# First weight loads in smaller pieces, and the squares and norm steps of the first projection moved back

## The chip, the cores and the metric

The kernel runs on one core of one Trainium2 chip, which has five engines: TensorE (PE in the profile; PEld is its weight load), VectorE (DVE), ScalarE (ACT), GpSimd (POOL) and SyncE (SP, which here only issues transfers). The metric is the time on the device in microseconds; lower is better.

## The reference

One layer of a streaming encoder over T = 1072 tokens in one list: 16 meta tokens, 1024 prompt frames, 32 frames of a running stream. What matters here is its beginning:

```python
def rmsnorm(x, g):
    r = rsqrt(mean(x * x, -1) + EPS)
    return (x * r) * g

z = rmsnorm(x, norm_mix) @ w_in              # (T, 1024) @ (1024, 1792)
a_in, q, k, v = split(z, [1024, 1536, 1664])
glu = a_in[:, :512] * sigmoid(a_in[:, 512:])
# depthwise conv (width 31) over glu, layer norm, swish   -> A
# sliding-window attention over q, k, v                   -> B
x = x + concat([A, B]) @ w_out
# then a gated feed-forward with a conv of width 3, a residual, and a last rmsnorm
```

All data is float32.

## The kernel before

**Layout.** Channels lie on the 128 partitions and tokens on the free axis, so x is 8 slices of 128 channels (k = 0 to 7), in three blocks of tokens, TB: block 0 has 336, block 1 384, block 2 352. w_in is cut into 14 chunks of 128 output columns, `win[c]`, each with 8 slices of 128 rows.

**Three products for one.** Each operand is split into a rounded high part and a remainder, both float32r: ACT makes the high part, DVE the remainder (`split` for weights, lines L246 and L247; L338 and L339 for x, which also multiply by the norm's gain). The tiles are `whi`, `wlo` for weights and `hi`, `lo` (HI[b], LO[b]) for x. A **step** is one slice k of one chunk and one block: three matmuls (L252 high by high, L253 high weight by low x, L254 low weight by high x). Eight steps in a row add up one chunk of one block in one PSUM bank.

**The first 48 steps.** `START` lists them: chunks 0 and 1 of block 0 step by step in turn (steps 0 to 15), then chunk 0 of block 1 (16 to 23), chunk 0 of block 2 (24 to 31), chunk 1 of block 1 (32 to 39), chunk 1 of block 2 (40 to 47). From step 48 on the main loop takes the other chunks, each for blocks 0, 1, 2; its first is chunk 2 (48 to 55 for block 0, 56 to 63, 64 to 71). A counter, `slot`, numbers the steps. Before step 0 PE runs WRM = 18 matmuls on ones (L319), which need no input. Three PSUM banks, tag `mm`, hold in turn chunk 0 and chunk 1 of block 0 and chunk 0 of block 1; tags `o`, `pt0` and `pt1` hold the other three sums. Step 48 takes the first `mm` bank again, once chunk 0 of block 0 has been read out.

**The norm comes late.** The projection runs on x times gain, and its result is multiplied by `rb[b]`, the tokens' 1/rms, on the way out of PSUM (DVE, L572 and the lines by it). For rb[b], ACT squares each slice of x (L359, into `sqs` buffers, six of them), DVE adds them up (L362), and `rms_first` runs in three parts, each called behind a step that `RM[b]` names: column sums by six PE instructions (L268, out `R`) with DVE and POOL work for the power -0.5 (L271, L275 to L279); three ACT multiplications into `diag` (L283); six PE instructions that spread the result (L289, out `R`) and an ACT copy into rb (L349).

**What sets the order.** PE's instructions follow the text. ACT's follow it from the main loop on; before that, ACT's, and DVE's, SP's and POOL's throughout, are put in order by a planner that takes what it thinks is ready, earlier in the text first. `tc.issue_after(ins)` puts an instruction behind `ins` on the same engine. `SQB[b]` = (b', k) puts block b's squares behind ACT's cast of slice k of block b', `SQD[b]` its additions behind DVE's remainder of that slice. Conv taps (L397, L400) fill DVE where nothing else is ready.

**Later weights.** A chunk from the main loop on comes by one transfer of 512 KB (L231); ACT writes the high part (L237) and the negated copy (L241), and a transfer that POOL issues adds the raw weights to that (L242). Chunks 0 and 1 own both buffers of `raw`, `whi` and `wlo`, so chunk 2 waits until chunk 0 is used up (step 31).

Of the kernel before, what the change touches and what calls it, by code (L numbers as in the profile page):

```python
# [18 lines left out]
P = 128  # L19
# [39 lines left out]
PF = 7  # L59
START = (((0, 0), (1, 0)), ((0, 1),), ((0, 2),), ((1, 1),), ((1, 2),))  # L60
WRM = 18
FS = 1
LASTK = ((0, 1), (1, 3), (3, 5), (5, 8))
ENDN = 448
# [36 lines left out]
DN = 264  # L101
FORD = (0, 1, *range(2, 10, 2), *range(3, 10, 2), *range(10, 18, 2), *range(11, 18, 2), 18, 19, 20, 21)
NSUM = 1
SQB = ((1, 7), (2, 7), (2, 7))
SQD = ((0, 7), (2, 7), (2, 7))
RM = ((27, 31, 41), (45, 48, 53), (56, 59, 63))
VR = 16
BW = SEG + 2 * NMETA
SSW = 128 + NS + NMETA + 1
# [14 lines left out]
def build():  # L124
# [35 lines left out]
    with tile.TileContext(nc, schedule_with_timeline_sim=True) as tc:  # L160
        with tc.tile_pool(name="cons", bufs=1) as cp, tc.tile_pool(name="wp", bufs=2) as wp, \
                tc.tile_pool(name="xp", bufs=1) as xp, tc.tile_pool(name="dr", bufs=1, space=DRAM) as dp:
            body(nc, tc, cp, wp, xp, dp, locals())
# [3 lines left out]
def body(nc, tc, cp, wp, xp, dp, io):  # L167
# [3 lines left out]
    d = _N()  # L171
# [18 lines left out]
    def pcol(name, i):  # L190
        o, _ = PRM[name]
        return prm[:, o + i:o + i + 1]
# [52 lines left out]
    def split(hi, lo, src):  # L245
        nc.scalar.copy(hi, src)  # L246
        nc.vector.tensor_tensor(out=lo, in0=src, in1=hi.bitcast(F32), op=ALU.subtract)  # L247
# [69 lines left out]
    hid, cast = {}, {}  # L317
    for i in range(WRM):
        nc.tensor.matmul(warm[:, 0:P], ones, ones, start=True, stop=True)  # L319

    nc.scalar.dma_start(prm, d.prm)
    for b, (t0, n) in enumerate(TB):
        if b == 0:
            pre = [[wp.tile([P, 1024], F32 if t == "raw" else F32R, tag=t, name=t) for t in ("raw", "whi", "wlo")]
                   for c in range(2)]
        for k in range(0, KD, 2):
            if b == 0 and k % 4 == 0:
                for c in range(2):
                    raw, hi, lo = (z[:, k * P:k * P + 512] for z in pre[c])
                    nc.sync.dma_start(raw, d.win[c, :, k:k + 4].rearrange("p a b -> p (a b)"))  # L330
                    split(hi, lo, raw)
            nc.sync.dma_start(X[b][:, k:k + 2, :], d.xT[:, k:k + 2, t0:t0 + n])
        if b == 0:
            pre = [z[1:] for z in pre]
        if b == 0:
            nc.scalar.dma_start(ident, d.cst[:, 0, :])
        for k in range(KD):
            hid[b, k] = nc.scalar.activation(HI[b][:, k, :], X[b][:, k, :], AF.Copy, scale=pcol("g1", k)).ins  # L338
            cast[b, k] = nc.vector.scalar_tensor_tensor(out=LO[b][:, k, :], in0=X[b][:, k, :], scalar=pcol("g1", k),  # L339
                                                        in1=HI[b][:, k, :].bitcast(F32), op0=ALU.mult,  # L340
                                                        op1=ALU.subtract).ins
# [11 lines left out]
    for b, (t0, n) in enumerate(TB):  # L353
        parts = [acc[:, p, t0:t0 + n] for p in (1, 0)[:NSUM]]
        for k in range(KD):
            sq = pd.tile([P, 384], F32, tag="sqs", name="sq", bufs=6)[:, :n]
            to = parts[k % NSUM] if k < NSUM else sq
            with tc.issue_after(hid[SQB[b]]):
                nc.scalar.activation(to, X[b][:, k, :], AF.Square)  # L359
            if k >= NSUM:  # L360
                with tc.issue_after(cast[SQD[b]]):
                    nc.vector.tensor_tensor(out=parts[k % NSUM], in0=parts[k % NSUM], in1=sq, op=ALU.add)  # L362
# [184 lines left out]
    def in_mm(b, w, lead=0):  # L547
# [3 lines left out]
        for k in range(KD):  # L551
            mm3(ps, [k], lambda k: hv[:, k, :], lambda k: lv[:, k, :], lambda k: HI[b][:, k, lead:],
                lambda k: LO[b][:, k, lead:], k == 0, k == KD - 1)
            for g, at in zip(rms1, RM):
                if slot[0] in at:
# [446 lines left out]
    a, z = None, None  # L1002
# [3 lines left out]
    for i in range(len(jobs) + 2):  # L1006
# [34 lines left out]
        z, a = a, job  # L1041
# [159 lines left out]
    with tc.tile_pool(name="psB", bufs=1, space=PSUM, reuse_waits="tile") as pf:  # L1201
# [346 lines left out]
        def d_mm(ps, w, rows, t0, n):  # L1548
            at = t0 - NMETA
            mm3(ps, range(len(rows)), lambda k: w[0][:, k * P:k * P + P], lambda k: w[1][:, k * P:k * P + P],  # L1550
                lambda k: rows[k][0][:, at:at + n], lambda k: rows[k][1][:, at:at + n])
# [141 lines left out]
        for pos, (t0, n) in enumerate(ENDS):  # L1693
            last = pos + 1 == len(ENDS)
            for m in range(KD):
                ps = mmt()[:, :n]
                d_mm(ps, [z[:, m % 2] for z in wend[m // 2]], crow, t0, n)
                if pos and FS <= m < FS + 3:
                    next(fin, None)
# [10 lines left out]
                elif m:  # L1710
                    parts.append(to)
                if pos and m >= FS + 3:
                    next(fin, None)
# [103 lines left out]
```

## Time and profile before

| | |
|---|---|
| median of 3 runs | 1063.87 us (1062.63 to 1065.57) |
| profiled execution, its own time | 1064.06 us |
| its span, first to last instruction | 1062.3 us |
| mean granted TensorE clock | 0.996 of full speed |
| PE busy | 1037.6 us, 98% of the span |
| DVE busy | 865.6 us, 81% |
| ACT busy | 508.6 us, 48% |

The span is what the rows' times count in; 1.8 us of the execution lie around it. PE's busy time is that of overlapping matmuls, so gaps are read from the starts of successive matmuls.

### The profile page before, as it was taken

To read this page: it belongs to the slowest core of one execution; us is meant where nothing else is said; L and a number is where in the kernel's file an instruction comes from. 1 tells how busy PE (TensorE), PEld (TensorE's weight loads), DVE (VectorE), ACT (ScalarE), POOL (GpSimd) and SP (SyncE) were. 2 spreads that over 40 slices of the span, in tenths; PEclk is the share of its full clock that TensorE was granted. 3 is DMA by queue.
4 is the path that set the end of the run, shared out by engine and by line. 5 is a ranking of instruction groups with operands and counts; after the bars stand their busy time and mean duration, and the time that the engine had idled before them with its cause. 6 is when DMAs were issued, how large, how long until landed. Compare 5 with 4: busy or idle time off the path is not lost.

```text
span 1062.3 us, 19939 instructions
## 1 busy us (share of the span) xinstructions
PE 1037.6 (98%) x7741; PEld 1010.0 (95%) x7741; DVE 865.6 (81%) x1643; ACT 508.6 (48%) x1068; POOL 173.4 (16%) x203
## 2 busy tenths in 40 slices
PE   9999999889999999999999999999999999999996
PEld 9999997658999999999999999999999999999996
DVE  7999997899978988878888887888778766985636
ACT  8653436897675644333333343443336622532333
POOL 1132120002335212001011000100102041000042
PEclk9999999999999999999999999999999999999998
DMA  7388772124953222242243234233226795732204
GB/s 265 89 172 168 148 151 65 41 54 70 172 148 107 68 83 90 74 129 92 71 130 103 72 105 127 62 102 116 87 81 185 245 201 122 245 122 80 61 6 159
DMA packets 69560, 123.88 MB, mean 117 GB/s; under 512 B 10449, under 2 KB 43465, under 8 KB 69465
## 3 DMA queue, kind: packets, MB, share of 16 engines
q1 hardware_dynamic: 57048, 97.44, 28.9%
q0 software_dynamic: 12128, 24.95, 14.0%
q8 instruction: 61, 1.00, 0.4%
q10 hardware_dynamic: 288, 0.22, 0.1%
q14 instruction: 35, 0.28, 0.1%
HBM read 78.90 MB, written 27.51 MB: 100 GB/s over the span
## 4 chain that ended last, share of the span: by engine, by line
PE 59%; DVE 5%; DMA 2%; ACT 1%; issue 1%; POOL 0%; SPq 0%; DVEq 0%; ACTq 0%; POOLq 0%
PE mm L1280 52%; PE mm L254 2%; PE mm L252 2%; PE mm L253 2%; DMA rb<-yq 2%; DVE traw L1297 1%; DMA yd<-x 1%; DVE x L1342 0%; DVE tl L1312 0%; ACT bh L1216 0%; PE R L289 0%; DVE wlo L1217 0%; POOL rb L297 0%; DVE bl L301 0%; ACT bh L300 0%
## 5 line engine op out<-in xcount | busy, mean ns | idle before, releaser
L1280 PE MATMUL mm<-bh,sl 128*128 128x264 f32 (+1 forms) x912 | 214.8, 285 | 0.3 <-ACT bh L1216 0.3
L1280 PEld LDWEIGHTS mm<-bh,sl 128*128 128x128 f32 x912 | 157.5, 189 | 0.5 <-ACT bh L1216 0.5
L400 DVE SCALAR_TENSOR_TENSOR acc<-glu,prm,acc 128x324 f32<-128x324 f32 (+4 forms) x190 | 155.2, 845 | 1.1
L1280 PE MATMUL mm<-bl,sl 128*128 128x264 f32 (+1 forms) x424 | 121.1, 286 | 0.9 <-DVE bl L1217 0.9
L1280 PE MATMUL mm<-th,rawr 128*128 128x266 f32 (+1 forms) x640 | 121.4, 285 | 0.0
L1280 PE MATMUL mm<-bh,wlo 128*128 128x264 f32 (+1 forms) x440 | 118.1, 285 | 0.0
L1417 DVE TENSOR_TENSOR x<-x,mm 128x264 f32<-128x264 f32 (+7 forms) x238 | 76.5, 348 | 50.0 <-PE mm L1280 49.9
L1280 PE MATMUL mm<-bh,whi 128*128 128x264 f32 (+1 forms) x440 | 113.4, 285 | 0.7 <-DVE x L1417 0.6
L252 PE MATMUL mm<-hi,whi 128*128 128x352 f32 (+3 forms) x312 | 103.9, 333 | 0.0
L1280 PEld LDWEIGHTS mm<-th,rawr 128*128 128x128 f32 x640 | 101.2, 189 | 0.0
L254 PE MATMUL mm<-hi,wlo 128*128 128x352 f32 (+3 forms) x312 | 101.1, 324 | 0.0
L253 PE MATMUL mm<-lo,whi 128*128 128x352 f32 (+3 forms) x312 | 101.1, 324 | 0.0
L1280 PE MATMUL mm<-th,sl 128*128 128x264 f32 (+1 forms) x352 | 92.8, 284 | 0.0
L1280 PE MATMUL mm<-tl,rawr 128*128 128x266 f32 (+1 forms) x320 | 91.4, 286 | 0.0
L1280 PEld LDWEIGHTS mm<-bl,sl 128*128 128x128 f32 x424 | 80.0, 189 | 1.1 <-DVE bl L1217 1.1
L1280 PEld LDWEIGHTS mm<-bh,wlo 128*128 128x128 f32 x440 | 80.6, 189 | 0.0
L1280 PEld LDWEIGHTS mm<-bh,whi 128*128 128x128 f32 x440 | 79.1, 189 | 1.1 <-DVE x L1417 0.8
L1280 PE MATMUL mm<-bl,whi 128*128 128x264 f32 (+1 forms) x272 | 77.6, 285 | 0.0
L1216 ACT CAST sl<-x 128x512 fp32r<-128x512 f32 (+1 forms) x41 | 29.7, 726 | 75.1 <-DMA x<-wup 36.8
L1280 PEld LDWEIGHTS mm<-th,sl 128*128 128x128 f32 x352 | 64.0, 188 | 0.0
L1280 PEld LDWEIGHTS mm<-tl,rawr 128*128 128x128 f32 x320 | 60.4, 189 | 0.0
L252 PEld LDWEIGHTS mm<-hi,whi 128*128 128x128 f32 x312 | 58.7, 188 | 1.0 <-issue 0.6
(362 smaller groups left out, 2934.2 us busy)
## 6 DMA issues: line engine op xcount, KB each, us to landing
x<-wup SPq DMA_DIRECT2D x20, 512.0 KB, 4.2
x<-wup SPq DMA_DIRECT2D x40, 256.0 KB, 2.7
yq<-x SPq DMA_DIRECT2D x32, 264.0 KB, 2.8
wlo<-raw POOLq DMA_DIRECT2D x16, 512.0 KB, 4.6
ca<-ca POOLq DMA_DIRECT2D x18, 383.0 KB, 5.2
raw<-win SPq DMA_DIRECT2D x12, 512.0 KB, 4.5
raw<-wdn SPq DMA_DIRECT2D x12, 512.0 KB, 3.5
rb<-yq SPq DMA_DIRECT2D x10, 528.0 KB, 4.5
```

The lines of the kernel that those rows point to most:

```text
L252: nc.tensor.matmul(ps, whi(k), xhi(k), start=first and i == 0, stop=False)
L253: nc.tensor.matmul(ps, whi(k), xlo(k), start=False, stop=False)
L254: nc.tensor.matmul(ps, wlo(k), xhi(k), start=False, stop=last and i == n - 1)
L400: nc.vector.scalar_tensor_tensor(out=a, in0=e[:, a0 + k:a1 + k], scalar=pcol("cw", p * CW + k), in1=a, op0=ALU.mult, op1=ALU.add)
L1216: nc.scalar.copy(hi, raw)
L1280: nc.tensor.matmul(ps, w[:, j, :], x[:, j, :], start=first and j + i == 0, stop=j == 3 and i == 2, skip_group_check=True)
L1297: nc.vector.scalar_tensor_tensor(out=out[:, lo_:hi_], in0=x, scalar=pcol("g2", k), in1=z[:, lo_:hi_], op0=ALU.mult, op1=ALU.subtract)
L1417: nc.vector.tensor_tensor(out=z, in0=z, in1=banks[k][:, lo_:hi_], op=ALU.add)
```

## The change

The first load of chunks 0 and 1 came in two pieces of four slices each; it now comes in three, of two, two and four slices, each pair of pieces ahead of the x slices from the same k on. Each piece has its transfer, its ACT cast and its DVE remainder. The squares of all blocks now stand behind the last cast of block 2, and the additions behind its last remainder. The norm's three parts are called behind later steps.

```diff
+WPRE = {0: 2, 2: 4, 4: 8}
...
-SQB = ((1, 7), (2, 7), (2, 7))
-SQD = ((0, 7), (2, 7), (2, 7))
-RM = ((27, 31, 41), (45, 48, 53), (56, 59, 63))
+SQB = ((2, 7), (2, 7), (2, 7))
+SQD = ((2, 7), (2, 7), (2, 7))
+RM = ((34, 37, 45), (50, 53, 57), (58, 61, 66))
...
         for k in range(0, KD, 2):
-            if b == 0 and k % 4 == 0:
+            if b == 0 and k in WPRE:
+                e = WPRE[k]
                 for c in range(2):
-                    raw, hi, lo = (z[:, k * P:k * P + 512] for z in pre[c])
-                    nc.sync.dma_start(raw, d.win[c, :, k:k + 4].rearrange("p a b -> p (a b)"))
+                    raw, hi, lo = (z[:, k * P:e * P] for z in pre[c])
+                    nc.sync.dma_start(raw, d.win[c, :, k:e].rearrange("p a b -> p (a b)"))
                     split(hi, lo, raw)
             nc.sync.dma_start(X[b][:, k:k + 2, :], d.xT[:, k:k + 2, t0:t0 + n])
```

## Rows read from the trace of the kernel before

**Rows 1.** Stretches: length, PE, PEld, DVE, ACT, POOL busy, clock, DMA share, GB/s.

```profile
0.00:50.00 50.00, 48.26 (x292) 46.28 (x293) 42.23 (x104) 36.88 (x76) 7.44 (x17) 1.00 0.60 187
...
200.00:250.00 50.00, 44.47 (x334) 32.61 (x333) 49.60 (x180) 47.19 (x153) 4.46 (x4) 1.00 0.20 38
```

**Rows 2.** Timeline of PE, 7 to 16 us: start, duration, instruction.

```profile
6.77 1.29 PE L319 MATMUL warm<-ones 128*128 128x128 f32 x10
7.82 0.40 PE L252 MATMUL mm<-hi,whi 128*128 128x336 f32 x1
...
15.31 0.34 PE L252 MATMUL mm<-hi,whi 128*128 128x384 f32 x1
```

**Rows 3.** Timeline of PE around the first steps of block 2.

```profile
19.48 0.32 PE L252 MATMUL o<-hi,whi 128*128 128x352 f32 x1
20.25 0.43 PE L253 MATMUL o<-lo,whi 128*128 128x352 f32 x1 [0.45 <-DVE lo L339]
...
21.18 0.32 PE L252 MATMUL o<-hi,whi 128*128 128x352 f32 x1
21.66 0.43 PE L253 MATMUL o<-lo,whi 128*128 128x352 f32 x1 [0.16 <-DVE lo L339]
```

**Rows 4.** Timeline of SP's queue: the first issues.

```profile
0.75 0.88 SPq L330 DMA_DIRECT2D raw<-win  x2
...
4.72 6.44 SPq L332 DMA_DIRECT2D xs<-xT  x10
```

**Rows 5.** Timeline of ACT: casts of x, squares, chunk 2's weights.

```profile
9.93 6.03 ACT L338 ACTIVATE hi<-xs,prm 128x336 fp32r<-128x336 f32 x12 [0.18 <-DMA xs<-xT]
...
16.24 2.34 ACT L359 ACTIVATE sq<-xs 128x336 f32<-128x336 f32 x6
18.48 2.01 ACT L338 ACTIVATE hi<-xs,prm 128x352 fp32r<-128x352 f32 x4
...
26.40 1.04 ACT L237 CAST whi<-raw 128x1024 fp32r<-128x1024 f32 x1
```

**Rows 6.** Timeline of DVE, the first remainders and additions.

```profile
9.27 1.29 DVE L247 TENSOR_TENSOR wlo<-raw,whi 128x512 fp32r<-128x512 f32 x2
10.55 6.24 DVE L339 SCALAR_TENSOR_TENSOR lo<-xs,prm,hi 128x336 fp32r<-128x336 f32 x12
16.74 2.96 DVE L362 TENSOR_TENSOR acc<-acc,sq 128x336 f32<-128x336 f32 x5
19.62 1.07 DVE L339 SCALAR_TENSOR_TENSOR lo<-xs,prm,hi 128x352 fp32r<-128x352 f32 x2
```

**Rows 7.** Timeline of PE: block 0's spread, block 1's sums, step 48.

```profile
30.39 0.83 PE L289 MATMUL R<-diag,ones 128*128 128x128 f32 x6
...
33.00 0.73 PE L268 MATMUL R<-ones,acc 128*128 128x1 f32 x6
33.59 0.41 PE L252 MATMUL pt<-hi,whi 128*128 128x352 f32 x1
...
34.64 0.31 PE L252 MATMUL mm<-hi,whi 128*128 128x336 f32 x1
```

**Rows 8.** Timelines of ACT and DVE behind that spread.

```profile
31.89 0.41 ACT L349 COPY rb<-R 128x336 f32<-128x336 f32 x1
...
32.64 0.50 DVE L572 TENSOR_TENSOR glu<-mm,rb 128x336 f32<-128x336 f32 x1
```

**Rows 9.** The same three links for block 1, from the timelines of PE, ACT and DVE.

```profile
37.41 0.83 PE L289 MATMUL R<-diag,ones 128*128 128x128 f32 x6
...
38.28 0.48 ACT L349 COPY rb<-R 128x384 f32<-128x384 f32 x1 [0.72 <-PE R L289]
...
38.79 0.97 DVE L572 TENSOR_TENSOR glu<-mm,rb 128x384 f32<-128x384 f32 x2 [0.16 <-ACT rb L349]
```

**Rows 10.** Timeline of POOL and of SP's queue: chunk 2's low part, and the load behind it.

```profile
28.70 0.95 POOL L242 DMA_DIRECT2D wlo<-raw  x1 [2.90 <-ACT wlo L241]
...
33.39 0.34 SPq L231 DMA_DIRECT2D raw<-win  x1
```

## The prediction

> **What bounds the kernel now.** I read the busy time by stretches first, then PE's timeline from its first matmul on, then the queues of ACT, DVE, SP and POOL beside it. In the first 50 us PE is busy for 48.3 and DVE for 42.2 [rows 1], so time is lost there only where PE's successive matmuls start further apart than they need. From 7.82 to 15.31 us PE starts 48 matmuls of 336 columns, 0.156 us apart [rows 2]: a step is 0.47 us, by the same rate 0.49 at 352 columns and 0.53 at 384 (my estimates). Up to step 24 nothing is lost. Then PE twice waits for the low part of block 2's x: 19.48 to 20.25 and 21.18 to 21.66, where 0.16 would do, so 0.61 and 0.32 us [rows 3]. The cause is in the other queues: ACT squares block 0 for 2.34 us before it casts block 2 from 18.48 on [rows 5], and DVE adds these squares from 16.74 to 19.62 before it makes block 2's first remainder [rows 6]. Later on PE isn't the only full engine: from 200 to 250 us DVE is busy for 49.6 of 50 and PE for 44.5 [rows 1], so what PE gains early need not all reach the end.
>
> **The first matmul.** The last ten warm-up instructions run from 6.77 us until the first real matmul starts at 7.82 [rows 2]. They stand in front of it on PE and are not changed, so earlier weights or an earlier first x slice gain nothing: 0, and a gain is excluded.
>
> **The weight pieces.** Two 256 KB transfers become four of 128 KB; four casts and four remainders of 512 columns become four of 256 and two of 512, each two more. Prices: a cast of 1024 columns takes 1.04 us [rows 5]; DVE's two remainders of 512 take 1.29, and twelve x remainders, of 368 columns on average, 6.24 [rows 6]. Between 0.645 at 512 and 0.52 at 368 columns, the part that doesn't shrink with the columns is about 0.2 us, so DVE has about 0.4 us more to do, and ACT I put at the same. The next work they could delay is x slice 4: its remainder starts at 10.55 and takes about 0.5, so it is there at 11.07, and PE asks for it with matmul 25, at 7.82 + 25 x 0.156 = 11.72. The room is 0.65 us, so the casts are covered. The two more issues on SP take 0.44 us each (two in 0.88) [rows 4] and put the x slices behind them back by 0.88 us of issuing. But SP's ten x issues take 6.44 us, 0.64 each [rows 4], more than issuing needs: they wait for transfers to land, and the bytes ahead of each x slice from 2 on are those of before. So I take 0. The upper bound is both in full, 0.88 + 0.4 - 0.65 = 0.63 us; none of this can gain.
>
> The Trainium skill speaks against this part: "DMA: Bandwidth & Descriptors", section "Anatomy of one DMA", gives every transfer a fixed cost of about 2 us, and the section on bandwidth wants at least 1 MiB in each. If two more transfers cost 4 us one after the other, slice 4 would come 3.4 us too late, and the time would be 1067.0. Ten transfers issued 0.64 us apart [rows 4] say that such costs overlap here.
>
> **Squares behind block 2's casts.** ACT can cast block 2 when block 1 is done, 9.93 + 6.03 = 15.96 us, and DVE follow from 10.55 + 6.24 = 16.79 on [rows 5, 6]. Eight remainders at 0.53 end by about 21.0; PE asks for the first at 19.64 and for the last at 23.1. Whether block 2's x has landed by 15.96 isn't shown; at 18.48 ACT did not wait for it [rows 5]. Even then the first remainder would be ready at about 19.65. So both stalls go: -0.93 us, at worst -0.6.
>
> **Block 0's sums at step 34.** They take the place of step 27, so PE comes to step 32 at 19.48 + 8 x 0.49 = 23.4 and through step 34 at 25.0. The seven additions now start behind the last remainder, at 21.0 to 21.4, and five take 2.96 us [rows 6], 0.59 each, so they end at 25.1 to 25.5. PE waits 0.1 to 0.5 us; I take 0.4. If block 2's x holds ACT up to 18.48, the end is 2 us later: bounds 0 and 2.2.
>
> **Block 0's read-out before step 48.** Step 48 needs the first `mm` bank, so the spread R, the copy on ACT and the read-out on DVE. Before, these took from 30.39 to 32.64 + 0.50 = 33.14 us, and PE came to step 48 at 34.64 [rows 7, 8]: 1.5 us to spare. Now R stands behind step 45 instead of 41, and block 1's sums, worth 0.59 (33.00 to 33.59) [rows 7], no longer lie in between. From the start of R to step 48 there remain two steps and R itself, 2 x 0.49 + 0.59 = 1.57 us. The same links of block 1 took 37.41 to 38.79 + 0.49, or 1.87 us, with ACT free; those of block 0 took 2.75, with ACT at its squares [rows 8, 9]. So PE waits 0.3 to 1.2 us. I take 0.3, since only the last squares can still be in ACT's way. R itself may find its `diag` late: ACT's casts from 20.0 to 20.5 on are followed by 24 squares of 0.39, two weight operations of about 1.04 and three small ones that I put at 1 us together, about 12.5 us, so all is done by 33.0 at the latest, against R at some 31.8: up to 1.2 us, and I take 0 because `diag` comes earlier in the text than the weights.
>
> **Blocks 1 and 2.** Block 1's sums and R lie seven steps apart instead of eight, block 2's eight instead of seven. From the sums' end at 33.73 to R at 37.41 block 1's chain had 3.7 us and R followed without a stated wait [rows 7, 9]; seven steps are about 3.4. I take the two as cancelling, bounds -0.3 and +0.3. The PE instructions only change places.
>
> **Chunk 2's weights.** ACT cast them at 26.40 [rows 5], POOL issued the low part at 28.70, and it had landed by 33.39, where the load that reuses its raw buffer is issued [rows 10]. PE now wants it at 34.64 - 0.93 - 0.59 + 0.31 = 33.43, plus 0.7 for the two waits above: covered with 0.7 us to spare, if ACT takes the weights no later than before. That order is the planner's and isn't in the trace.
>
> **Sum.** -0.93 + 0.4 + 0.3 = -0.23 us. The span goes from 1062.3 to 1062.1, the execution's own time from 1064.06 to 1063.8. That execution lies 0.19 above the median of 1063.87, so on the median I expect 1063.6.
>
> **Rivals.**
> - *All of the gain.* x lands early, ACT and DVE are free, neither step 34 nor 48 waits: -0.93, 1062.9. For it: block 1's chain needs only 1.87. Against: the additions alone end 0.1 us too late.
> - *Chunk 2's weights late (the other side).* ACT puts them behind all squares and `diag`: 20.5 + 24 x 0.39 + 1.0 = 30.9 instead of 26.40. The low part lands 4.5 us later, at 37.9, and step 48 waits 37.9 - 33.8 = 4.1: -0.93 + 0.4 + 4.1 = +3.6, 1067.4. For it: squares stand earlier in the text. Against: ACT has only six buffers to run ahead of DVE, so it must pause and take something else, and chunk 2's weights are ready from step 31 on, at about 23.4. It makes the kernel slower from 27.3 us on, and by over 0.3% from about 30.6.
> - *The norm chain late.* Step 34 at 2.2, R at 1.2, step 48 at 0.3: +2.8, 1066.6.
> - *The pieces cost.* Two landings of 0.64 and 0.4 of casts, less the room of 0.65: 1.0 us, 1064.6.
> - *Another order later on.* The sums of blocks 1 and 2 are read out one chunk later, so taps move on DVE, which is full from 200 to 250 us. That stretch has 5.5 us of PE idle [rows 1]; a share of it either way, some 4 us at most.
>
> **How the numbers follow.** A measurement can tell 0.3%, 3.2 us, from no change. Forecast 0.50 (1062.5 to 1064.8), all of the gain 0.13, weights late 0.09, chain late 0.08, pieces 0.06, another order 0.14 (half each side). Slower by over 0.3%: half of weights late, a fifth of chain late, a third of another order's slower half, 0.09; faster: 0.06, most of another order's faster half. The rest, 0.85, is no change. The range from 1061.3 to 1066.4 leaves out the far weights case and the ends of another order.
>
> **What would show it.** Right: the first matmul still at about 7.8 us; no wait for `lo` at block 2's first steps; the sums behind step 34 and step 48 starting within 0.5 us of their neighbours; step 48 at about 33.5. Wrong: a gap before R, or before the third matmul of step 48 with L237 after 27 us; a gap at step 8; or an early gain lost again by 250 us.

## The result, and the profile after

| | before | after |
|---|---|---|
| median | 1063.67 us (12 runs) | 1066.62 us (12 runs, 1064.9 to 1067.43) |
| ratio | | 1.0025, 95% interval 1.0017 to 1.0033 |
| profiled execution, own time | 1064.06 us | 1066.45 us |
| its span | 1062.3 us | 1064.7 us |

By the ratio the kernel became 0.25% slower, which is 2.7 us (the medians lie 2.95 us apart). Forecast were 1063.6 us and a range up to 1066.4; the median lies 0.2 us outside it. In the new kernel the numbers of lines are one higher up to the loads (L253 to L255 are the three matmuls, L269 the sums, L284 `diag`, L290 the spread) and two higher behind them (L340 and L341 the casts, L361 the squares, L364 the additions, L351 the copy into rb, L574 the read-out, L576 the sigmoid).

The stretches of the new kernel answer to [rows 1]: length, PE, PEld, DVE, ACT, POOL busy, clock, DMA share, GB/s.

```profile
0.00:50.00 50.00, 46.15 (x283) 44.22 (x284) 38.85 (x96) 35.55 (x75) 7.55 (x17) 1.00 0.60 187
200.00:250.00 50.00, 44.64 (x334) 32.55 (x333) 49.45 (x181) 45.36 (x148) 3.28 (x3) 1.00 0.19 38
```

The later stretch is as it was. In the first 50 us PE is busy for 46.15 instead of 48.26 and DVE for 38.85 instead of 42.23, so the loss is there, and it is waiting, not work. PE's timeline of the new kernel (start, duration, instruction, and the idle time before it with what ended it) answers to [rows 2, 3, 7, 9]:

```profile
7.06 0.42 PE L253 MATMUL mm<-hi,whi 128*128 128x336 f32 x1 [0.25 <-ACT hi L340]
7.66 0.42 PE L254 MATMUL mm<-lo,whi 128*128 128x336 f32 x1 [0.18 <-DVE lo L341]
...
11.33 0.32 PE L253 MATMUL mm<-hi,whi 128*128 128x336 f32 x1
11.67 0.42 PE L254 MATMUL mm<-lo,whi 128*128 128x336 f32 x1
...
19.50 0.32 PE L253 MATMUL o<-hi,whi 128*128 128x352 f32 x1
19.65 0.33 PE L254 MATMUL o<-lo,whi 128*128 128x352 f32 x1
...
25.97 0.83 PE L269 MATMUL R<-ones,acc 128*128 128x1 f32 x6 [0.90 <-DVE acc L364]
...
32.23 0.83 PE L290 MATMUL R<-diag,ones 128*128 128x128 f32 x6
32.82 0.41 PE L253 MATMUL pt<-hi,whi 128*128 128x352 f32 x1
...
34.43 0.42 PE L253 MATMUL mm<-hi,whi 128*128 128x336 f32 x1 [0.40 <-DVE glu L574]
...
35.93 0.73 PE L269 MATMUL R<-ones,acc 128*128 128x1 f32 x6
...
41.20 1.07 PE L290 MATMUL R<-diag,ones 128*128 128x128 f32 x6 [1.04 <-ACT diag L284]
42.02 0.42 PE L253 MATMUL mm<-hi,whi 128*128 128x384 f32 x1
...
64.16 0.42 PE L255 MATMUL mm<-hi,wlo 128*128 128x336 f32 x1 [0.23 <-DMA wlo<-raw]
```

Both stalls for block 2's `lo` are gone. In their place stand four waits: for block 0's additions (25.97), for its read-out (34.43), for block 1's `diag` (41.20) and for chunk 4's low part (64.16). I compared the start of each step with that of the same step before. Up to step 9 the difference is +0.04 us, although this execution's first matmul started 0.76 us sooner: PE loses that lead waiting for `lo`, 0.47 us in step 0 and 0.30 in step 8 (11.33 to 11.67). Then block 2's stalls give -1.15, step 34's sums +1.06, step 48 +0.67, block 1's spread +1.47, block 2's -0.09, chunk 4 +0.49. Together that is +2.49, and step 130 starts at 82.74 us instead of 80.25. So nearly all of the 2.4 us by which the span grew is lost before 65 us, and the largest part is a wait that was forecast at nothing.

What made block 1's `diag` late is to be seen in the queues of ACT, DVE and POOL. ACT:

```profile
19.87 1.07 ACT L340 ACTIVATE hi<-xs,prm 128x352 fp32r<-128x352 f32 x2 [0.52 <-DMA xs<-xT]
...
31.86 1.25 ACT L361 ACTIVATE sq<-xs 128x352 f32<-128x352 f32 x3
33.10 0.44 ACT L351 COPY rb<-R 128x336 f32<-128x336 f32 x1
33.90 1.05 ACT L238 CAST whi<-raw 128x1024 fp32r<-128x1024 f32 x1 [0.36 <-PE pt L254]
34.85 1.06 ACT L242 ACTIVATE wlo<-raw 128x1024 fp32r<-128x1024 f32 x1
35.93 1.28 ACT L576 ACT_TABLE_LOAD   x1
37.22 0.49 ACT L576 ACTIVATE glu<-glu 128x336 f32<-128x336 f32 x1
40.74 0.99 ACT L284 ACTIVATE diag<-ident,stat 128x128 f32<-128x128 f32 x3 [3.03 <-DVE stat L280]
```

DVE and then POOL:

```profile
21.72 4.20 DVE L364 TENSOR_TENSOR acc<-acc,sq 128x336 f32<-128x336 f32 x7
...
30.80 3.16 DVE L364 TENSOR_TENSOR acc<-acc,sq 128x384 f32<-128x384 f32 x6
33.87 0.50 DVE L574 TENSOR_TENSOR glu<-mm,rb 128x336 f32<-128x336 f32 x1
...
37.74 0.51 DVE L633 TENSOR_TENSOR glu<-glu,rb 128x336 f32<-128x336 f32 x1 [1.97 <-ACT glu L576]
38.17 0.15 DVE L272 TENSOR_SCALAR stat<-R 128x3 f32<-128x3 f32 x1
```

```profile
38.41 0.91 POOL L276 TENSOR_TENSOR stat<-stat,mhalf 128x3 f32<-128x3 f32 x1 [1.28 <-DVE stat L272]
```

Block 0's copy and read-out come about 1.2 us later than in [rows 8]. The order of ACT has turned over with them: chunk 3's weights (L238, L242) now stand ahead of the table load and block 0's sigmoid; before, the sigmoid came first and ended at 34.10. ACT in the kernel before:

```profile
33.62 0.48 ACT L574 ACTIVATE glu<-glu 128x336 f32<-128x336 f32 x1
34.68 1.05 ACT L237 CAST whi<-raw 128x1024 fp32r<-128x1024 f32 x1 [0.57 <-PE pt L253]
```

So the sigmoid now starts at 37.22. DVE has the product L633 next and waits 1.97 us for it. Block 1's first norm step (L272), whose column sums were done at 36.66, is queued behind that product and starts at 38.17; POOL, DVE and ACT follow in turn, and `diag` starts at 40.74.

### The profile page after: what moved, and what is told of

Its sections match the earlier page's. It is cut to its first block, busy times and chain, and to the rows that moved or that the text cites. A ratio compares the mean times of both kernels' runs of the same rounds, so it can differ in the third digit from the quotient of the medians.

```text
span 1064.7 us, 19943 instructions
## 1 busy us (share of the span) xinstructions
PE 1038.1 (98%) x7741; PEld 1010.0 (95%) x7741; DVE 865.9 (81%) x1645; ACT 509.6 (48%) x1070; POOL 163.8 (15%) x203
## 4 chain that ended last, share of the span: by engine, by line
PE 60%; DVE 4%; ACT 2%; DMA 1%; issue 1%; POOL 0%; DVEq 0%; ACTq 0%; SPq 0%; POOLq 0%
PE mm L1282 53%; PE mm L255 2%; PE mm L253 2%; PE mm L254 2%; DMA rb<-yq 1%; DVE traw L1299 1%; DMA raw<-wdn 1%; DVE tl L1314 0%; ACT bh L1218 0%; DVE wlo L1219 0%; POOL rb L298 0%; DVE bl L302 0%; ACT bh L301 0%; PE R L290 0%; DVE x L1344 0%
## 5 line engine op out<-in xcount | busy, mean ns | idle before, releaser
L402 DVE SCALAR_TENSOR_TENSOR acc<-glu,prm,acc 128x1090 f32<-128x1090 f32 (+4 forms) x190 | 154.9, 845 | 1.0
L253 PE MATMUL mm<-hi,whi 128*128 128x352 f32 (+3 forms) x312 | 104.7, 336 | 0.7 <-DVE glu L574 0.4
L255 PE MATMUL mm<-hi,wlo 128*128 128x352 f32 (+3 forms) x312 | 101.7, 326 | 0.2 <-DMA wlo<-raw 0.2
L253 PEld LDWEIGHTS mm<-hi,whi 128*128 128x128 f32 x312 | 59.1, 189 | 2.2 <-DVE glu L574 0.7
```

The source lines that it names most:

```text
L253: nc.tensor.matmul(ps, whi(k), xhi(k), start=first and i == 0, stop=False)
L255: nc.tensor.matmul(ps, wlo(k), xhi(k), start=False, stop=last and i == n - 1)
L402: nc.vector.scalar_tensor_tensor(out=a, in0=e[:, a0 + k:a1 + k], scalar=pcol("cw", p * CW + k), in1=a, op0=ALU.mult, op1=ALU.add)
```

## The experiments

Each was run 5 to 12 times, next to runs of the kernel before on the same chip; an interval that holds 1 means that the run isn't told from before. "Early shift" is read from the one profile of each: how much later than in the kernel before step 130 starts, less the same for step 9 (for e6, step 58 less step 9). It leaves out the first steps (and with them what the pieces cost there), whose start differs from execution to execution: step 9 began between 11.83 and 12.39 us in kernels with the very opening of the kernel before.

| run | what differs | median us (before) | ratio, 95% interval | early shift us |
|---|---|---|---|---|
| after | | 1066.62 (1063.67) | 1.0025, 1.0017 to 1.0033 | +2.45 |
| e1 | before + pieces | 1065.03 (1063.75) | 1.0013, 1.0004 to 1.0021 | +2.07 |
| e2 | after without pieces | 1066.67 (1063.75) | 1.0027, 1.0016 to 1.0038 | +3.59 |
| e3 | after, blocks 1, 2's norm back | 1065.72 (1063.75) | 1.0023, 1.0014 to 1.0031 | +1.51 |
| e4 | after, sigmoid first | 1065.79 (1063.75) | 1.0016, 1.0008 to 1.0024 | +1.07 |
| e5 | before + norm steps | 1066.50 (1064.10) | 1.0022, 1.0013 to 1.0031 | +3.50 |
| e6 | before + squares | 1069.73 (1064.10) | 1.0049, 1.0036 to 1.0061 | +7.03 |
| e7 | after, block 0's sums at 36 | 1065.71 (1064.10) | 1.0016, 1.0007 to 1.0025 | +1.66 |
| e8 | squares, other steps, sigmoid first | 1064.95 (1064.10) | 1.0004, 0.9995 to 1.0013 | +1.17 |
| e9 | before + blocks 1, 2's norm later | 1066.93 (1063.58) | 1.0031, 1.0019 to 1.0043 | +2.65 |
| e10 | before + block 0's norm later | 1064.63 (1063.58) | 1.0007, 0.9998 to 1.0016 | +1.02 |
| e11 | after with the edits of e3 and e4 | 1064.18 (1063.31) | 1.0006, 0.9997 to 1.0015 | -0.07 |
| e12 | e9, block 1's spread two steps later | 1064.20 (1063.31) | 1.0007, 0.9999 to 1.0016 | +0.63 |

**e1, the pieces alone.**

```diff
+WPRE = {0: 2, 2: 4, 4: 8}
...
-            if b == 0 and k % 4 == 0:
+            if b == 0 and k in WPRE:
```

> The kernel before with the smaller weight pieces alone; squares and norm steps as before. Theory (the norm steps' new places cost the time): x slice 4 is late by some 0.3 us at step 8, and nothing else changes much, so 1063.4 to 1064.3. Rival (the pieces and their two more transfers cost it, by making all of x later): 1065.5 or more, with waits for x spread over steps 8 to 31.

1065.03 us, 1.3 us slower, between the two ranges. Step 9 starts only 0.05 us later than before. But ACT casts block 2's x 0.5 us later (from 18.98 us instead of 18.48 [rows 5]), and PE's first wait for block 2's `lo` grows from 0.45 us [rows 3] to 0.70. Later the order on ACT changes as well: chunk 2's negated copy goes behind block 0's `diag`, and step 48 waits for the low part. ACT's and PE's timelines of this kernel:

```profile
29.60 0.99 ACT L284 ACTIVATE diag<-ident,stat 128x128 f32<-128x128 f32 x3
30.49 1.05 ACT L242 ACTIVATE wlo<-raw 128x1024 fp32r<-128x1024 f32 x1
```

```profile
20.75 0.43 PE L254 MATMUL o<-lo,whi 128*128 128x352 f32 x1 [0.70 <-DVE lo L341]
...
36.49 0.42 PE L255 MATMUL mm<-hi,wlo 128*128 128x336 f32 x1 [0.89 <-DMA wlo<-raw]
```

The wait at step 48 is the mechanism of the rival "chunk 2's weights late", in a kernel where I hadn't looked for it, and at about a quarter of its 4.1 us. The whole change does not show it: there ACT cast these weights at 24.64 us.

**e2, all but the pieces.** The same lines the other way round, in the changed kernel.

> The changed kernel with the first weights in two pieces again. Theory: the waits before block 0's sums, at step 48 and before block 1's spread are there as in the changed kernel, so 1066.0 to 1066.7. Rival (the pieces cost it): 1063.5 to 1064.5.

1066.67 us, as the whole change, so on top of the rest the pieces cost and gain nothing that the time can tell. In the trace they do: without them ACT goes on with block 2's last x slices at 19.31 us instead of 19.87, and block 0's additions start at 21.16 instead of 21.72. PE still waits for them behind step 34 (0.85 us), since DVE makes eight additions in a row here, one more than block 0 has. The read-out stands behind block 1's additions on DVE here (step 48 waits 1.60 us for it) and block 1's spread waits only 0.58: the waits trade places.

**e3, norm steps of blocks 1 and 2 back.**

```diff
-RM = ((34, 37, 45), (50, 53, 57), (58, 61, 66))
+RM = ((34, 37, 45), (45, 48, 53), (56, 59, 63))
```

> The changed kernel with the norm steps of blocks 1 and 2 back at their old places (block 0's stay late). Theory (block 1's first small DVE operation stood behind a product that waits for the sigmoid, because its sums come five steps later): it stands ahead of that product again, the 1.5 us before block 1's spread go, and perhaps the 0.5 for chunk 4's weights: 1064.6 to 1065.2. Rival (block 1's chain is late because its squares are): 1066.3 to 1066.8.

1065.72 us, between the two ranges, and by its ratio (1.0023) not told from the whole change. The wait at block 1's spread stays, 0.92 us. ACT in this kernel:

```profile
35.69 1.05 ACT L242 ACTIVATE wlo<-raw 128x1024 fp32r<-128x1024 f32 x1
36.75 1.28 ACT L576 ACT_TABLE_LOAD   x1
38.05 0.48 ACT L576 ACTIVATE glu<-glu 128x336 f32<-128x336 f32 x1
38.44 0.97 ACT L284 ACTIVATE diag<-ident,stat 128x128 f32<-128x128 f32 x3
```

DVE had finished block 1's norm at 36.2 us; `diag` stands without a gap behind chunk 3's weights, the table load and the sigmoid. So DVE's queue is not the root here: the jam is on ACT.

**e4, sigmoid first.** ACT's instructions of chunk 3's weights (and of later chunks, which come later anyway) are put behind block 0's first sigmoid.

```diff
-                        nc.scalar.activation(g, g, AF.Sigmoid)
+                        sig.append(nc.scalar.activation(g, g, AF.Sigmoid).ins)
...
-        w, nxt = nxt, take()
+        with tc.issue_after(sig[0]):
+            w, nxt = nxt, take()
```

> The changed kernel with chunk 3's two weight operations on ACT queued behind the first sigmoid; nothing else is changed. Theory (the sigmoid stood 2 us behind these weights on ACT, and DVE with block 1's small operation behind the sigmoid): the sigmoid ends some 2 us sooner, DVE's idle of 2.0 us before that product shrinks to under 0.5, and the wait before block 1's spread from 1.2 to under 0.3 us: 1064.8 to 1065.5. Rival (the chain of block 1 itself is too long for seven steps): no change, 1066.3 to 1066.8.

1065.79 us, between the two ranges; the intervals of its ratio and of the whole change's overlap. The sigmoid starts at 35.09 and the wait at block 1's spread is gone: R starts at 40.22 with no idle time stated. The waits at steps 34 and 48 stay (0.86 and 0.40). Block 1's sums still stand behind step 50, seven steps ahead of R. On POOL the power now comes ahead of the issue of chunk 3's low part, and the chain from sums to spread takes 40.22 - 36.17 = 4.05 us. PE, then POOL:

```profile
36.17 0.73 PE L269 MATMUL R<-ones,acc 128*128 128x1 f32 x6
...
40.22 0.91 PE L290 MATMUL R<-diag,ones 128*128 128x128 f32 x6
```

```profile
37.18 0.99 POOL L276 TENSOR_TENSOR stat<-stat,mhalf 128x3 f32<-128x3 f32 x1 [3.59 <-DVE stat L272]
38.13 0.91 POOL L243 DMA_DIRECT2D wlo<-raw  x1
```

**e5, the norm steps alone; e6, the squares alone.** Each is one of the two constants in the kernel before.

> The kernel before with the norm steps at their new places alone; weight pieces and squares as before. Theory (the late norm steps bring waits of their own, at step 48 and before block 1's spread): block 2's two stalls stay, 0.9 us, block 0's sums don't wait, step 48 waits 0.5 to 1.5 us and block 1's spread 1 to 1.5: 1065.5 to 1066.5. Rival (the late norm steps cost something only because the squares are late): 1063.5 to 1064.2.

> The kernel before with the squares and additions behind block 2's casts alone; norm steps at their old places, weights in two pieces. Theory (block 0's additions end at about 25.9 us whatever step asks for them): PE comes to the sums behind step 27 at about 21.5 and waits some 4 us; block 2's stalls of 0.9 us go; block 0's read-out is then early enough for step 48, and block 1's small operation ahead of the sigmoid's product: 1065.5 to 1067. Rival (the additions are done sooner if nothing else comes between): under 1064.5.

e5, 1066.50 us: nearly the whole loss without the new place of the squares; block 2's stalls stay (0.53 and 0.17), and block 1's spread waits 1.28; step 48, where I expected 0.5 to 1.5, has no stated wait. With the sums moved away from step 27 a third stall for `lo` shows behind the two (0.16): the sums had hidden it. e6, 1069.73 us, the worst and 2.7 us above the range expected: behind step 27 the sums wait 4.37 us for the additions, as expected, but PE is slow behind that wait (the last section has it). Its stretches, columns as above:

```profile
20.00:27.00 7.00, 2.63 (x16) 2.34 (x14) 6.06 (x12) 7.00 (x19) 0.00 (x0) 0.92 0.26 71
27.00:33.00 6.00, 6.00 (x22) 6.00 (x23) 5.24 (x14) 5.60 (x11) 1.15 (x1) 0.52 0.01 1
33.00:40.00 7.00, 7.00 (x48) 7.00 (x46) 1.49 (x7) 2.90 (x6) 1.15 (x3) 1.00 0.56 126
```

So the squares' new place needs the sums' new place, and that brings the rest with it.

**e7, block 0's sums two steps later.** In the changed kernel:

```diff
-RM = ((34, 37, 45), (50, 53, 57), (58, 61, 66))
+RM = ((36, 39, 45), (50, 53, 57), (58, 61, 66))
```

> The changed kernel with block 0's sums behind step 36 and its diag behind step 39 instead of 34 and 37; its spread stays behind 45. Theory (the chain from the last addition to the read-out sets the time at step 48, and the place of the sums doesn't): the wait of 1.06 us before the sums goes, and as much appears at the spread or at step 48: 1066.2 to 1066.8. Rival (each wait is lost for itself): 1065.4 to 1065.8.

1065.71 us, in the rival's range, though by the ratio not told from the whole change. The trace bears out the theory: the wait for the additions is gone, but step 48 waits 0.97 us for the read-out instead of 0.40; the end of block 0's chain doesn't move with its sums. Block 1's spread waits 0.48 instead of 1.04.

**e8, an attempt at a better version.** The kernel before with the squares moved, the sigmoid first, and

```diff
-RM = ((27, 31, 41), (45, 48, 53), (56, 59, 63))
+RM = ((36, 39, 45), (47, 50, 54), (57, 60, 64))
```

> Weights in two pieces, squares behind block 2's casts, block 0's norm steps at 36, 39, 45, block 1's at 47, 50, 54, block 2's at 57, 60, 64, and chunk 3's weight operations on ACT behind the first sigmoid. Theory: block 2's stalls and block 1's wait go, and what is left is the wait for block 0's read-out at step 48, 1 to 1.5 us more than was gained: 1064.3 to 1065.2. Rival (the waits were each the work of one order alone): 1063.0 or less.

1064.95 us, not told from the kernel before, and no better. The stalls' 1.15 us go into smaller waits: 0.55 at block 0's spread, 0.56 at block 2's, the rest at the steps beside them.

**e9 and e10, which block's norm is it?** By then my theory was that block 0's later spread is the one root.

```diff
-RM = ((27, 31, 41), (45, 48, 53), (56, 59, 63))
+RM = ((27, 31, 41), (50, 53, 57), (58, 61, 66))   # e9
+RM = ((34, 37, 45), (45, 48, 53), (56, 59, 63))   # e10
```

> The kernel before with the norm steps of blocks 1 and 2 alone moved, (50, 53, 57) and (58, 61, 66); block 0's stay at 27, 31 and 41. If block 0's later spread is the cause of the loss (its copy, read-out and sigmoid come behind chunk 3's weights on ACT, which then makes block 1's norm late), nothing is lost here: no wait at step 48, the sigmoid ahead of chunk 3's weights, 1063.3 to 1064.7 us. If the later steps of blocks 1 and 2 are the cause, most of the loss of the run with all three blocks' steps moved (1066.5 us) is here: 1065.5 to 1066.5 us, with the wait at block 1's spread.

> The kernel before with block 0's norm steps alone moved, from (27, 31, 41) to (34, 37, 45). If block 0's later spread is the cause, this loses 1 to 2 us, 1065 to 1066 us: a wait of 0.4 to 0.9 us at step 48 for block 0's read-out, and block 1's spread or chunk 4's first step late behind it. If the later steps of blocks 1 and 2 are the cause, this loses at most 0.5 us: 1063.5 to 1064.6 us, step 48 within 0.3 us of its neighbours.

As the one root it fell. e9, with block 0 untouched and the sigmoid in time, takes 1066.93 us, and e10 1064.63, which isn't told from before (its early shift is 1.02 us, 0.5 of it at block 1's spread). In e10 block 0's spread is as late as in the changed kernel, and yet the sigmoid (35.46) comes ahead of chunk 3's weights (35.85). In e9 step 48 has no wait, but block 1's spread has. Its chain, from the timelines of PE, DVE and POOL:

```profile
35.79 0.73 PE L268 MATMUL R<-ones,acc 128*128 128x1 f32 x6
...
41.16 1.07 PE L289 MATMUL R<-diag,ones 128*128 128x128 f32 x6 [1.18 <-ACT diag L283]
```

```profile
36.63 0.15 DVE L271 TENSOR_SCALAR stat<-R 128x3 f32<-128x3 f32 x1
...
38.66 0.16 DVE L276 SCALAR_TENSOR_TENSOR stat<-stat 128x3 f32<-128x3 f32 x1 [0.17 <-POOL stat L275]
38.97 0.51 DVE L572 TENSOR_TENSOR glu<-mm,rb 128x336 f32<-128x336 f32 x1 [0.15 <-PE mm L254]
...
40.45 0.16 DVE L279 SCALAR_TENSOR_TENSOR stat<-stat 128x3 f32<-128x3 f32 x1
```

```profile
36.75 0.86 POOL L242 DMA_DIRECT2D wlo<-raw  x1 [4.09 <-ACT wlo L241]
37.33 1.30 POOL L275 TENSOR_TENSOR stat<-stat,mhalf 128x3 f32<-128x3 f32 x1
```

POOL in the kernel before:

```profile
34.01 0.89 POOL L275 TENSOR_TENSOR stat<-stat,mhalf 128x3 f32<-128x3 f32 x1 [1.79 <-DVE stat L271]
```

From sums to spread it takes 5.37 us; in the kernel before it took 37.41 - 33.00 = 4.41 [rows 7, 9], in e4 4.05, both without a stated wait of PE. In e9, with its sums behind step 50, the chain meets other work. On POOL the issue of chunk 3's low part stands ahead of the power, which starts 0.55 us after the end of DVE's first step and takes 1.30; before it was 0.1 and 0.89. From DVE's first step to its second it is 2.03 us instead of 1.35, and from the second to the last 1.79 instead of 1.07, with a read-out of block 0 between them (38.97). And the seven steps to R give only 41.16 - 35.79 - 1.18 = 4.19 us.

**e11 and e12, both reasons removed, and more room.** e11 is the changed kernel with the edits of e3 and e4 together. e12 is e9 with

```diff
-RM = ((27, 31, 41), (50, 53, 57), (58, 61, 66))
+RM = ((27, 31, 41), (50, 53, 59), (58, 61, 66))
```

> The changed kernel with block 1's and 2's norm steps back at (45, 48, 53) and (56, 59, 63) and chunk 3's weights put behind block 0's first sigmoid on ACT. Theory now: block 1's spread waits for either of two reasons, its sums standing only seven steps ahead (room 4.0 us, chain 4.05 us at best), or chunk 3's weights standing ahead of the sigmoid and of diag on ACT; here both are gone. So no wait at block 1's spread; what is left is the stalls' gain of 1.15 us against the waits behind step 34 (1.1) and at step 48 (0.4 to 0.7): 1063.6 to 1065.0 us. Rival: what costs lies elsewhere (the pieces, a later order), and it stays at 1065.5 to 1067 us.

> The kernel before with block 1's norm at (50, 53, 59) and block 2's at (58, 61, 66): the last kernel with two more steps (1.05 us) of room before block 1's spread. If the wait there (1.2 us, and 0.24 us of refilling) is the chain's length against its room, it shrinks to 0.1 to 0.4 us and the time falls by about 1 us, to 1065.3 to 1066.3 us. If the chain comes late by whatever room it gets, the wait stays over 0.8 us and the time at 1066.5 to 1067.3 us.

e11: 1064.18 us, ratio 1.0006, no longer told from the kernel before, and its interval ends below that of the whole change. In its profile block 1's spread follows without a stated wait, at 37.21 against 37.41 before [rows 9], and step 130 starts within 0.01 us of before:

```profile
32.46 0.73 PE L269 MATMUL R<-ones,acc 128*128 128x1 f32 x6
...
37.21 1.01 PE L290 MATMUL R<-diag,ones 128*128 128x128 f32 x6
```

The other waits are smaller too: 0.42 us for the additions instead of 0.90, none stated at step 48, where block 1's sums stand behind R again, and none for chunk 4's low part.

e12: 1064.20 us, ratio 1.0007. Two steps more of room and the wait is gone; the ratio falls by 0.24% against e9, 2.5 us, where I expected 1: block 2's wait goes as well, and what PE loses right behind a wait. What is left in it is one wait for chunk 4's low part:

```profile
40.94 0.83 PE L289 MATMUL R<-diag,ones 128*128 128x128 f32 x6
...
62.20 0.42 PE L254 MATMUL mm<-hi,wlo 128*128 128x336 f32 x1 [0.86 <-DMA wlo<-raw]
```

No version is faster than the kernel before.

## Why the prediction was wrong

**What bounds the kernel** was right: the loss came from PE's starts in the first 65 us, and 200 to 250 us stayed as it was.

**The first matmul.** "A gain is excluded" was wrong as put: it started at 7.06 us instead of 7.82, since the warm-ups ended sooner (36 instructions in 5.74 us instead of 7.00), and then waited for `hi` and `lo`. But this isn't the change's doing (the opening of e12 is that of the kernel before, and its first matmul started at 7.23), and by step 9 nothing of it was left: 0, as taken.

**The weight pieces.** 0 was taken and 0.04 us measured at step 9, but that is luck in part. PE did wait at step 8, 0.30 us, the sign of being wrong that the prediction names; this execution's early start paid for it. Without the pieces e2, which started at 7.12, has no such wait and comes to step 9 at 11.83 instead of 12.09. What was wrong is the premise that x isn't put back: the first x remainder behind the weights came 0.5 us later (11.05 against 10.55 in [rows 6]), and SP's ten x issues took 6.96 us instead of 6.44 [rows 4]. Beyond slice 4 that delay stays in the queues of ACT and DVE: it lengthens the wait for block 2's `lo` in e1, and in the whole change it makes block 0's additions late. The step also left out that two more casts can turn over the planner's order 20 us later, as in e1. The sum by the fixed cost in the Trainium skill ("DMA: Bandwidth & Descriptors", "Anatomy of one DMA"), slice 4 being 3.4 us late, isn't borne out here: its remainder was 0.5 us late. That section gives the cost for transfers that GpSimd issues, and these come from SyncE.

**Squares behind block 2's casts.** Right: both stalls went, and gave 1.15 instead of 0.93 us, since each stall also cost about 0.1 us right behind it.

**Block 0's sums.** The term of 0.4 us was 1.06, within its bounds of 0 and 2.2. The additions began at 21.72 instead of 21.0 to 21.4 and ended at 25.92. ACT waited 0.52 us for block 2's last x slices (until 19.87), the case I named and gave no weight. It waits for them without the pieces too, but only until 19.31 (e2) or 19.53 (e6), against 19.43 to 20.11 in the five profiles with pieces and moved squares. In e2 the additions begin at 21.16, as forecast. So the later start here is mostly the pieces' delay of x, as far as single profiles can tell; that e2 waits nevertheless is the work of the extra addition.

**Block 0's read-out.** The term of 0.3 us was 0.67. From R to step 48 it took 34.43 - 32.23 = 2.2 us. ACT's copy stood behind the last squares (until 33.1), as I had named, and DVE's read-out behind the additions (until 33.9), which I had not put in.

**Blocks 1 and 2: the step that failed.** "I take the two as cancelling, bounds -0.3 and +0.3": block 1's spread cost 1.47 us. I had set what the chain had before, 3.7 us from the sums' end, against seven steps. But its length is set by its neighbours, and they change with its place. Two groups of neighbours made it late, each enough by itself: chunk 3's weights on ACT ahead of sigmoid and `diag` (e3 keeps this one: 0.92 us); and, behind step 50, the issue of chunk 3's low part on POOL and a read-out on DVE ahead of its links, a chain of 5.4 us in 4.2 us of room (e9 keeps this one: 1.18 us). The place alone isn't enough: e4 keeps it, with both groups out of the way, and its chain of 4.05 us is in time. That the wait goes with the neighbours is shown by e4 and e11, and e12 shows that room alone suffices. In e11 2.0 of the 2.7 us go, but the waits at step 34, at step 48 and for chunk 4 shrink as well, so not all of the 2.0 is this wait.

Block 2's part didn't cancel it either. Its spread was a little late in the kernel before, with seven steps (R at 44.07, 0.40 us behind the last matmul, and the next one 0.83 behind R, where 0.17 and 0.59 would do: 0.47 us). With eight steps it still is (R at 47.48, 0.28 and 0.82): only 0.09 us came back.

**Chunk 2's weights** came in time, as taken. The next chunk whose weights could be late, chunk 4 (0.49 us), was not looked at; ACT cast them at 55.54 us instead of 51.62.

**The sum and the rivals.** -0.93 + 0.4 + 0.3 + 0 was in truth -1.15 + 1.06 + 0.67 + 1.47 and some +0.4. "The norm chain late" gave 1066.6, nearly the time measured, and named steps 34 and 48 rightly, but that it fits is luck: it had 2.2 us at step 34, where 1.06 were lost, and its third wait was block 0's spread, which had none. It had a chance of only 0.08 because I took the chains of blocks 1 and 2 out of it. "The pieces cost" gave 1.0 us; alone they cost 1.3 (e1), but mostly through ACT's order. The bound for "no change" (0.3%) held with 0.25%, though the interval reaches 0.33%.

**What stays open.** Why the pieces turn over ACT's order when alone and not with the rest. What puts chunk 3's weights ahead of the sigmoid on ACT: block 0's later spread alone doesn't (e10); with the squares moved (e3) or the other blocks' norm steps late (e5) it does. And how much of an early shift reaches the end: it ranks the runs about as the medians do, but single ones stand off by up to 1 us (e3 and e5 lie on either side), and profiles of single executions can't tell more.

## What to carry to other kernels

When a step of a chain is moved in kernels whose engines work in a fixed order, write out for every link what will stand ahead of it on its engine at the new place (issues of transfers on POOL, a table load, the next weights), and add that up; the chain's old duration says little there: the same chain took 4.05, 5.27 and 5.37 us with its sums behind step 50, by what stood ahead of its links. Give a chain that crosses four engines room for the worst of its neighbours: two steps of room (e12) took away most of a loss of 3.3 us. And look past the wait that is removed to the next thing in each queue: what fills the gap may be something that used to come later.

## What the runs showed of the hardware

Two things I had not expected. In e6 PE waited 4.37 us up to 25.90, after full work; from 27.20 to 32.76 us it then started 18 matmuls 0.29 us (352 columns) and 0.32 us (384 columns) apart, instead of 0.16 and 0.17. The granted clock was 0.92 in 20 to 27 us, 0.52 in 27 to 33, nearly all of it at the lower level of 1.2 GHz, and 1.00 from 33 on. That took 5.56 us instead of some 3.0, so the wait of 4.4 us cost about 2.6 more. None of the waits of up to 1.6 us in the other runs was followed by such a stretch; there the granted clock was 1.00 in all stretches up to 100 us.

And a wait of PE costs a little more than its idle time. In the changed kernel block 0's sums, which had waited, take 0.69 us to the next matmul (25.97 to 26.66), block 1's, which hadn't, 0.59 (35.93 to 36.52); a single matmul that had waited takes 0.26 (34.43 to 34.69) instead of 0.16. So about 0.1 us is to be added to such a wait. Behind the spread that had waited it is more, 0.82 us (41.20 to 42.02) instead of 0.59 (32.23 to 32.82), but part of that is still waiting: the six instructions use three `diag`, which ACT finishes one after the other, the last at 41.73.
